# w_down by Strassen's seven products, and the sums of a second block moved from GpSimd to VectorE and ScalarE

## The chip, the cores and the metric

One Trainium2 chip, one of its cores. The metric is the device time of one execution in microseconds (us). Five engines work side by side, each through its own queue in order: TensorE (PE in the profile, its weight loads PEld), VectorE (DVE), ScalarE (ACT), GpSimd (POOL) and SyncE (SP), which issues the DMAs.

## The reference, cut to what matters

Two transformer blocks on 1024 tokens of width 1024, all in float32. The first block has two layers with windowed attention and an mLSTM and is not touched by the change. The second block mixes four branches, projects them, and ends in a feed-forward with squared ReLU:

```
y_a = diff_attention(q, k, v); y_b = conformer_conv(hb)
y_c = fourier_mix(hc);         y_d = spatial_gate(hd)
x   = x + concat(y_a, y_b, y_c, y_d) @ w_out
xn2 = rmsnorm(x, norm2_g)
x   = x + square(relu(xn2 @ w_up)) @ w_down     # 1024x1024 @ 1024x4096, then @ 4096x1024
out = rmsnorm(x, final_g)
```

## The kernel before, in words

Every float32 matrix product is made of three matmuls on split operands (`mm3`, lines 244 to 247): a value is cut into a high part, rounded by ScalarE to a reduced float32 type (line 250, or 266 for weights), and a low part, the difference, which VectorE subtracts (line 251, or 267). In `weights` the subtraction goes to GpSimd while `self.wpool` is set.

The second block's mixers are `block2`. `conformer_conv` (line 1505) is 60 VectorE multiply-adds over 1024 elements, fed in the background of the projections. `fourier_dft8` (1685, 1695) and `fourier_out` (1713) make the butterflies of the Fourier branch on GpSimd; the results are split for matmuls (251, into `xc`). `wpool` is set from the start of `block2`. `diff_attention` has 32 steps (4 heads by 8 query blocks): scores, a masked maximum on VectorE (1924), exp on ScalarE (1926), and in `diff_combine` the difference of two softmaxes: a scalar (1935) and then, in 16 of the 32 steps (`COMBINE`), a scaling (1937) and an add (1938) on GpSimd, in the others one VectorE instruction (1940). `stacks` (1798) makes 16 copies, half on ScalarE and half on GpSimd (`STACK`).

The feed-forward is `block3`. `up` multiplies by w_up with Strassen's seven products: tokens and hidden columns are cut in two, and the table `UP` lists for each product m which blocks of tokens and of weights are added or subtracted and to which of the four output blocks (token half, column half) the result goes with which sign. A product is 8 units (j) of 24 matmuls, 128x128 by 128x512. The sums of weights (2042) and of tokens (2026) are made on GpSimd, and the weights of the next unit are prepared while a unit is multiplied (`ahead`). Results gather in SBUF, the first by a ScalarE copy (2076), later ones by a VectorE add from PSUM (2079); a finished block goes through ReLU and square (2083, 2084) and to the DRAM tensor `hd` (2085).

`down` multiplies by w_down directly: two token halves (t), 16 pairs of 128 hidden columns (f), and for each pair 4 row tiles by 2 column halves by 2 by 3 = 48 matmuls of 128x512 into 8 PSUM banks. Per pair SP loads 512 KB of `hd` (2100) and twice 512 KB of w_down (2106); three operands of 128x1024 are split. Then the residual `x4` is loaded, PSUM is added (2139), and `rms_row` (470, 465, 1383) makes the output, which is stored (2141).

```
for t in range(2):
    ps = [self.pg.get() for _ in range(8)]
    for f in range(0, 32, 2):
        o = operands(t, f)
        ...
        for tt in range(4):
            for c in range(2):
                product(ps[2 * tt + c], o, tt, c)
```

The raw operands of `up` and `down` pass through `raw`, a ring of 6 buffers of 128x1024 (2 in `fa`, 4 in `t816a`), in order: a load into a buffer waits for the last reader of that buffer; `hd` has two buffers of its own in `down`. The split operands lie in 3 slots (`rwh`, `rwl`) and, for w_down, 4 pairs in `xa`.

What sets the order of the work: `block2`, `block3` and the projection before them stand in `tc.block(schedule_with_timeline_sim=True)`. A planner simulates the engines at build time and writes each engine's queue from the instructions that are ready; during execution every queue runs strictly in that order.

Of the kernel before, what the change touches and what calls it, by code (L numbers as in the profile page):

```python
# [73 lines left out]
STACK = "apap"  # L74
# [117 lines left out]
class Kernel:  # L192
# [1244 lines left out]
    def block2(self):  # L1437
# [9 lines left out]
        self.wpool = True  # L1447
# [24 lines left out]
        self.rate = 0  # L1472
        self.ph, self.pg, self.pt = self.banks(0), self.banks(1), self.banks(2, 3)
# [207 lines left out]
    def fourier_dft8(self, X):  # L1681
# [3 lines left out]
        TT = lambda o, a, b, op: nc.gpsimd.tensor_tensor(o, a, b, op=op)  # L1685
# [9 lines left out]
        TS = lambda o, a, x: nc.gpsimd.tensor_scalar(o, a, x, 0.0, op0=ALU.mult, op1=ADD)  # L1695
# [14 lines left out]
    def fourier_out(self, Sf, yT):  # L1710
        nc = self.nc
        ADD, SUB = ALU.add, ALU.subtract
        TT = lambda o, a, b, op: nc.gpsimd.tensor_tensor(o, a, b, op=op)
# [70 lines left out]
    def stacks(self, h, m, out):  # L1784
# [144 lines left out]
    def diff_combine(self, d):  # L1929
# [87 lines left out]
    def up_tokens(self, m):  # L2017
# [13 lines left out]
    def up_weights(self, m, j, raw):  # L2031
# [9 lines left out]
        if op:  # L2041
            self.nc.gpsimd.tensor_tensor(rs[0].ap, rs[0].ap, rs[1].ap, op=op)  # L2042
# [4 lines left out]
    def up(self, cur, raw, ahead):  # L2047
        nc, V = self.nc, self.nc.vector
        self.pg = self.banks(0, 1, 2, 3, 4, 5, 6, 7)
        cs = self.T(0, 512, 36, Slots)  # L2050
# [4 lines left out]
        acc = {}  # L2055
        units = [(m, j) for m in range(7) for j in range(8)]
        nxt = None
        for i, (m, j) in enumerate(units):
            if i + 1 < len(units):
                ahead.append(self.up_weights(*units[i + 1], raw))  # L2060
# [5 lines left out]
            w = ahead.pop(0)  # L2066
            for a in range(2):
# [4 lines left out]
                f = 2 * j + a  # L2072
                for c, sign in self.UP[m][4]:
                    if (c, f) not in acc:
                        acc[c, f] = [cs.get(), left[c]]
                        nc.scalar.activation(acc[c, f][0].ap, p.ap, AF.Copy, scale=float(sign))  # L2076
                    else:
                        o = acc[c, f][0].ap
                        V.tensor_tensor(o, o, p.ap, op=ALU.add if sign > 0 else ALU.subtract)  # L2079
                    acc[c, f][1] -= 1  # L2080
                    if not acc[c, f][1]:
                        o = acc.pop((c, f))[0]
                        nc.scalar.activation(o.ap, o.ap, AF.Relu)  # L2083
                        nc.scalar.activation(o.ap, o.ap, AF.Square)  # L2084
                        nc.sync.dma_start(self.hd[16 * c[1] + f, :, c[0] * 512:c[0] * 512 + 512], o.ap)
                        cs.free(o)
            self.done([w])

    def down(self, raw):

        nc, V, A = self.nc, self.nc.vector, self.A
        rw = Ring(self.xa, [4096 + 1024 * i for i in range(4)] + [1024 * i for i in range(4)], 1024)
        rres = self.T(0, 1024, 4)
        self.rny = self.F(1024, 1024, 2)
        fg = self.F(0, 1024, 1).get()
        nc.sync.dma_start(fg.ap, A["final_g_2"].unsqueeze(0).broadcast_to([128, 1024]))

        def operands(t, f):
            r = self.rraw.get([128, 2, 512])
            nc.sync.dma_start(r.ap, self.hd[f:f + 2, :, t * 512:t * 512 + 512].rearrange("f p t -> p f t"))  # L2100
            hid = self.rwh.get([128, 2, 512]), self.rwl.get([128, 2, 512])
            self.split(hid[0].ap, hid[1].ap, r.ap)
            ws = []
            for i in range(2):
                r = raw.get()
                nc.sync.dma_start(r.ap, A["w_down_2"][0][(f + i) * 128:(f + i) * 128 + 128])
                w = rw.get(), rw.get()
                self.split(w[0].ap, w[1].ap, r.ap)
                ws.append(w)
            return f, hid, ws  # L2110

        def product(p, o, tt, c):
            f, (hh, hl), ws = o
            ts, cols = slice(tt * 128, tt * 128 + 128), slice(c * 512, c * 512 + 512)
            for i, (wh, wl) in enumerate(ws):
                self.mm3(p.ap, hh[:, i, ts], hl[:, i, ts], wh[:, cols], wl[:, cols], f + i == 0, f + i == 31)

        for t in range(2):
            ps = [self.pg.get() for _ in range(8)]
            last = []  # L2120
            for f in range(0, 32, 2):
                o = operands(t, f)
                if f >= 28 and t == 1:
                    last.append(o)
                    continue
                for tt in range(4):
                    for c in range(2):
                        product(ps[2 * tt + c], o, tt, c)
                self.done([o[1]])
            for tt in range(4):  # L2130
                rows = slice(t * 512 + tt * 128, t * 512 + tt * 128 + 128)
                x = rres.get()
                nc.sync.dma_start(x.ap, self.x4[rows])
# [60 lines left out]
```

## Time and profile before

| what | value |
|---|---|
| median of 3 runs | 2839.69 us (2837.2 to 2842.19) |
| the profiled execution | 2835.86 us; span of its profile 2834.1 us |
| PE busy | 2666.5 us, 94% |
| DVE, ACT, POOL busy | 1723.9, 1410.3, 725.0 us |
| DMA | 307.99 MB, mean 109 GB/s |

How to read the rows: in rows of windows a stretch is followed by its length, then busy us and (instructions) of PE, PEld, DVE, ACT and POOL, the granted TensorE clock (1.00 is the upper of its two levels, 2.4 GHz; 0.5 would be the lower, 1.2 GHz; a value between is a mix over the stretch), the DMA engines' busy share and GB/s. Matmuls are pipelined, so the time of one in a full stream is the stretch divided by their number, not the duration shown for one.

### The profile page before, as it was taken

How to read it: one execution, taken by the hardware profiler on the slowest of the kernel's cores; microseconds unless marked ns; L12 is line 12 of the kernel's file. 1: busy time of each engine (PE TensorE's matmuls, PEld its weight loads, DVE VectorE, ACT ScalarE, POOL GpSimd, SP SyncE). 2: the span in 40 equal slices, each digit the busy share in tenths (PEclk: the TensorE clock that was granted, in tenths of full speed). 3: DMA queues.
4: the chain of work that ended last, by engine and by line, in shares of the span. 5: the costliest groups of instructions: out<-in, count | busy, mean ns of one | idle time of the engine just before them, and what ended most of it. 6: DMA issues, size and time to landing. Idle time of an engine off the chain costs nothing. (4 is left out here: it accounts for less than half of the span.)

```text
span 2834.1 us, 44013 instructions
## 1 busy us (share of the span) xinstructions
PE 2666.5 (94%) x16414; PEld 2312.6 (82%) x16414; DVE 1723.9 (61%) x3530; ACT 1410.3 (50%) x3039; POOL 725.0 (26%) x810
## 2 busy tenths in 40 slices
PE   7999989999999999999998887898899999999998
PEld 3888878898889787888988877688798887888887
DVE  4788755646756788666455469788824475633433
ACT  4666545546525666556463252476705626632332
POOL 0122203414200122123131149265501544200000
PEclk9999999999999999999999988999999999999999
DMA  7101021112554101112215440423235666854542
GB/s 246 29 15 56 26 56 46 51 50 77 166 181 146 49 23 50 32 51 67 61 58 158 132 148 23 128 96 101 84 98 169 209 201 217 295 174 138 208 142 89
DMA packets 285859, 307.99 MB, mean 109 GB/s; under 512 B 17904, under 2 KB 242508, under 8 KB 285388
## 3 DMA queue, kind: packets, MB, share of 16 engines
q1 hardware_dynamic: 285644, 305.17, 34.1%
q8 instruction: 129, 2.11, 0.3%
q14 instruction: 86, 0.70, 0.1%
HBM read 249.70 MB, written 55.42 MB: 108 GB/s over the span
## 5 line engine op out<-in xcount | busy, mean ns | idle before, releaser
L245 PE MATMUL psum<-xa 128*128 128x512 f32 (+2 forms) x2200 | 779.8, 356 | 13.4 <-ACT xa L250 6.7
L246 PE MATMUL psum<-xa 128*128 128x512 f32 (+2 forms) x2200 | 775.4, 353 | 4.3 <-POOL xa L267 3.0
L247 PE MATMUL psum<-xa 128*128 128x512 f32 (+2 forms) x2200 | 773.4, 352 | 5.4 <-DVE xa L251 4.6
L245 PEld LDWEIGHTS psum<-xa 128*128 128x128 f32 x2200 | 421.6, 192 | 68.6 <-ACT xa L250 7.7
L247 PEld LDWEIGHTS psum<-xa 128*128 128x128 f32 x2200 | 421.3, 191 | 58.8 <-DVE xa L251 6.6
L246 PEld LDWEIGHTS psum<-xa 128*128 128x128 f32 x2200 | 421.9, 192 | 56.5 <-POOL xa L267 3.2
L465 POOL TENSOR_TENSOR rsb<-rsa,half 128x1 f32<-128x1 f32 (+1 forms) x129 | 90.0, 698 | 780.8 <-DVE rsa L463 723.5
L245 PE MATMUL psum<-xa,xg 128*128 128x256 f32 (+1 forms) x864 | 248.8, 288 | 1.7 <-DVE fa L1523 1.1
L247 PE MATMUL psum<-xa,xg 128*128 128x256 f32 (+1 forms) x864 | 245.7, 284 | 0.0
L246 PE MATMUL psum<-xa,xg 128*128 128x256 f32 (+1 forms) x864 | 245.7, 284 | 0.0
L251 DVE TENSOR_TENSOR xa<-fa,xa 128x1024 fp32r<-128x1024 f32 (+2 forms) x121 | 139.2, 1162 | 165.3 <-ACT xa L250 165.1
L806 POOL TENSOR_SCALAR fa<-fa,esk 128x640 f32<-128x640 f32 (+2 forms) x144 | 112.2, 792 | 450.9 <-DVE esk L804 361.2
L251 DVE TENSOR_TENSOR xa<-t816a,xa 128x1024 fp32r<-128x1024 f32 x84 | 115.1, 1372 | 175.5 <-ACT xa L250 171.9
L266 ACT ACTIVATE xa<-fa 128x1024 fp32r<-128x1024 f32 (+1 forms) x104 | 109.9, 1059 | 189.2 <-PE psum L247 109.9
L250 ACT ACTIVATE xa<-fa 128x1024 fp32r<-128x1024 f32 (+2 forms) x121 | 112.4, 942 | 171.5 <-PE psum L247 63.7
L267 DVE TENSOR_TENSOR xa<-fa,xa 128x1024 fp32r<-128x1024 f32 (+1 forms) x84 | 103.2, 1230 | 125.3 <-ACT xa L266 120.9
L250 ACT ACTIVATE xa<-t816a 128x1024 fp32r<-128x1024 f32 x84 | 88.3, 1054 | 167.4 <-PE psum L247 108.2
L245 PEld LDWEIGHTS psum<-xa,xg 128*128 128x128 f32 x864 | 163.9, 190 | 3.0 <-DVE fa L1523 1.5
L246 PEld LDWEIGHTS psum<-xa,xg 128*128 128x128 f32 x864 | 163.6, 189 | 0.7 <-issue 0.7
L247 PEld LDWEIGHTS psum<-xa,xg 128*128 128x128 f32 x864 | 163.5, 189 | 0.4 <-issue 0.3
L245 PE MATMUL psum<-xg,xa 128*128 128x512 f32 x376 | 154.1, 411 | 1.3 <-ACT xa L266 0.5
L247 PE MATMUL psum<-xg,xa 128*128 128x512 f32 x376 | 152.0, 405 | 2.7 <-POOL xa L267 2.7
(498 smaller groups left out, 6023.9 us busy)
## 6 DMA issues: line engine op xcount, KB each, us to landing
fa<-in_w_in_dram SPq DMA_DIRECT2D x64, 512.0 KB
t816a<-in_w_up_dram SPq DMA_DIRECT2D x64, 512.0 KB
fa<-in_w_ada_dram SPq DMA_DIRECT2D x48, 512.0 KB
t816a<-in_w_down_dram SPq DMA_DIRECT2D x44, 512.0 KB
fa<-in_w_up_dram SPq DMA_DIRECT2D x32, 512.0 KB
hd<-t816a SPq DMA_DIRECT2D x64, 256.0 KB
fa<-hd SPq DMA_DIRECT2D x32, 512.0 KB
fa<-in_w_out_dram SPq DMA_DIRECT2D x24, 512.0 KB
```

The costliest lines, as they stand in the source:

```text
L245: mm(out, lh, rh, start=start, stop=False)
L246: mm(out, lh, rl, start=False, stop=False)
L247: mm(out, ll, rh, start=False, stop=stop)
L250: self.nc.scalar.activation(hi, src, AF.Copy)
L251: self.nc.vector.tensor_tensor(lo, src, hi.bitcast(F32), op=ALU.subtract)
L266: self.nc.scalar.activation(h.ap, r.ap, AF.Copy)
L267: (self.nc.gpsimd if self.wpool else self.nc.vector).tensor_tensor(l.ap, r.ap, h.ap.bitcast(F32), op=ALU.subtract)
L465: self.nc.gpsimd.tensor_tensor(r, e, self.half.broadcast_to([128, m]), op=ALU.pow)
L806: nc.gpsimd.tensor_scalar(P[j][:, :nk], P[j][:, :nk], e[:, j:j + 1], 0.0, op0=ALU.mult, op1=ALU.add)
```

## The change

Five things. (1) `down` uses the seven products of the table `DOWN` (token halves and hidden halves; hidden halves and output-column halves): 7 products of 8 units of 24 matmuls into 4 banks each. A unit has one hidden factor and one weight factor of 128x1024, each possibly a sum of two blocks made on VectorE; two units are prepared ahead. (2) The hidden blocks of the second token half stay in SBUF (`self.H`); only the first half goes to `hd`. (3) The residual is loaded whole into `x`, and every product's result is added to the one or two places that its table row names. (4) In `up` the sums of weights and tokens move from GpSimd to VectorE, and the weights are prepared two units ahead instead of one; the accumulators are pairs of 512 columns. (5) In the second block the Fourier sums go to VectorE and its scalings to ScalarE, the low parts of weights before the attention to VectorE, half of the stack copies to ScalarE, the softmax scaling of 16 steps to ScalarE, and a VectorE instruction with two tensor inputs (1935) becomes one with one.

```diff
-STACK = "apap"
@@ block2
-        self.wpool = True
         next(zin[0])
...
         self.rate = 0
+        self.wpool = True
         self.ph, self.pg, self.pt = self.banks(0), self.banks(1), self.banks(2, 3)
@@ fourier_dft8 and fourier_out
-        TT = lambda o, a, b, op: nc.gpsimd.tensor_tensor(o, a, b, op=op)
+        TT = lambda o, a, b, op: nc.vector.tensor_tensor(o, a, b, op=op)
-        TS = lambda o, a, x: nc.gpsimd.tensor_scalar(o, a, x, 0.0, op0=ALU.mult, op1=ADD)
+        TS = lambda o, a, x: nc.scalar.activation(o, a, AF.Copy, scale=x)
@@ stacks
-            if STACK[h] == "a":
-                nc.scalar.activation(s[:96], f[:96], AF.Copy)
-            else:
-                nc.gpsimd.tensor_scalar(s[:96], f[:96], 1.0, 0.0, op0=ALU.mult, op1=ALU.add)
+            nc.scalar.activation(s[:96], f[:96], AF.Copy)
@@ diff_combine
-        V.scalar_tensor_tensor(r[:, 1:2], sm[:, 0:1], r[:, 1:2], self.nlam, op0=ALU.mult, op1=ALU.mult)
+        V.tensor_scalar(r[:, 1:2], r[:, 1:2], sm[:, 0:1], self.nlam, op0=ALU.mult, op1=ALU.mult)
-            nc.gpsimd.tensor_scalar(P[1].ap, P[1].ap, r[:, 1:2], 0.0, op0=ALU.mult, op1=ALU.add)
+            nc.scalar.activation(P[1].ap, P[1].ap, AF.Copy, scale=r[:, 1:2])
@@ up_tokens and up_weights
-                self.nc.gpsimd.tensor_tensor(r.ap, *src, op=op)
+                self.nc.vector.tensor_tensor(r.ap, *src, op=op)
-            self.nc.gpsimd.tensor_tensor(rs[0].ap, rs[0].ap, rs[1].ap, op=op)
+            self.nc.vector.tensor_tensor(rs[0].ap, rs[0].ap, rs[1].ap, op=op)
@@ up
+        ahead.append(self.up_weights(*units[1], raw))
-            if i + 1 < len(units):
-                ahead.append(self.up_weights(*units[i + 1], raw))
+            if i + 2 < len(units):
+                ahead.append(self.up_weights(*units[i + 2], raw))
...
+                    if c[0]:
+                        self.H[c, j] = o
+                    else:
+                        f = 16 * c[1] + 2 * j
+                        nc.sync.dma_start(self.hd[f:f + 2].rearrange("f p t -> p f t"), o.ap)
+                        self.cs.free(o)
+    DOWN = [
+        ([(0, 0), (0, 1)], ALU.add, [(1, 1)], None, [((0, 0), -1), ((0, 1), 1)]),
+        ([(0, 0)], None, [(0, 1), (1, 1)], ALU.subtract, [((0, 1), 1), ((1, 1), 1)]),
+        ([(0, 0), (1, 1)], ALU.add, [(0, 0), (1, 1)], ALU.add, [((0, 0), 1), ((1, 1), 1)]),
+        ([(0, 1), (1, 1)], ALU.subtract, [(1, 0), (1, 1)], ALU.add, [((0, 0), 1)]),
+        ([(1, 1)], None, [(1, 0), (0, 0)], ALU.subtract, [((0, 0), 1), ((1, 0), 1)]),
+        ([(1, 0), (1, 1)], ALU.add, [(0, 0)], None, [((1, 0), 1), ((1, 1), -1)]),
+        ([(1, 0), (0, 0)], ALU.subtract, [(0, 0), (0, 1)], ALU.add, [((1, 1), 1)]),
+    ]
@@ down
+        def factor(rs, op, h, l):
+            if op:
+                r = rs[0][0] if rs[0][1] else rs[1][0] if rs[1][1] else raw.get([128, 2, 512])
+                V.tensor_tensor(r.ap, rs[0][0].ap, rs[1][0].ap, op=op)
+            else:
+                r = rs[0][0]
+            self.split(h.ap, l.ap, r.ap)
...
+            for i in range(2):
+                self.mm3(p.ap, hh[:, i, ts], hl[:, i, ts], wh[:, i], wl[:, i], j + i == 0, j == 7 and i == 1)
+        units = [(m, j) for m in range(7) for j in range(8)]
+        ahead = [operands(*u) for u in units[:2]]
...
+                for (t, n), sign in self.DOWN[m][4]:
+                    y = x[4 * t + tt][:, n * 512:n * 512 + 512]
+                    V.tensor_tensor(y, y, ps[tt].ap, op=ALU.add if sign > 0 else ALU.subtract)
+                if m in (4, 6):
+                    t = 4 * (m == 6) + tt
+                    self.rms_row(x[t].ap, fg.ap)
+                    nc.sync.dma_start(A["out"][t * 128:t * 128 + 128], x[t].ap)
```

`operands(m, j)` loads each hidden block with t = 0 from `hd` and each weight block (256 rows by 512 columns) into a buffer of `raw`, 512 KB a load, and calls `factor` for the hidden and the weight side. A hidden block with t = 1 comes from `self.H` without a load.

## Rows read from the trace of the kernel before

**Rows 1.** The page, part 1: busy time, share of the span, instructions.
```profile
PE 2666.5 (94%) x16414; PEld 2312.6 (82%) x16414; DVE 1723.9 (61%) x3530; ACT 1410.3 (50%) x3039; POOL 725.0 (26%) x810
```
**Rows 2.** Windows: start of block 2, attention, up, down, and one full stretch of down.
```profile
1680.00:1800.00 120.00, 100.94 (x532) 87.02 (x530) 114.80 (x84) 34.76 (x80) 83.41 (x47) 0.91 0.15 46
...
1720.00:1840.00 120.00, 92.87 (x461) 77.73 (x460) 104.80 (x103) 40.44 (x83) 70.77 (x47) 0.87 0.27 84
1860.00:2060.00 200.00, 178.96 (x1336) 163.24 (x1335) 161.36 (x314) 138.22 (x256) 114.00 (x79) 0.97 0.29 88
2160.00:2480.00 320.00, 313.33 (x1362) 257.32 (x1362) 182.68 (x198) 175.63 (x264) 125.72 (x50) 0.98 0.69 224
2480.00:2826.00 346.00, 346.00 (x1528) 286.42 (x1526) 127.52 (x122) 101.76 (x110) 3.86 (x7) 1.00 0.44 150
...
2500.00:2600.00 100.00, 100.00 (x443) 82.84 (x442) 34.71 (x30) 30.84 (x31) 0.00 (x0) 1.00 0.44 148
```
**Rows 3.** Groups by line, VectorE, from 2480 us on (count, busy, mean ns).
```profile
L251 DVE TENSOR_TENSOR xa<-fa,xa 128x1024 fp32r<-128x1024 f32 x50 | 60.3, 1222 | 111.4 <-ACT xa L250 111.4
...
L2139 DVE TENSOR_TENSOR t816a<-t816a,psum 128x512 f32<-128x512 f32 x16 | 10.7, 685 | 9.2 <-PE psum L247 9.2
L1383 DVE SCALAR_TENSOR_TENSOR t816a<-t816a,rsb,fa 128x1024 f32<-128x1024 f32 x8 | 10.2, 1280 | 1.5 <-POOL rsb L465 1.5
```
**Rows 4.** The same stretch, ScalarE: the high parts.
```profile
L250 ACT ACTIVATE xa<-fa 128x1024 fp32r<-128x1024 f32 x50 | 51.6, 1050 | 121.3 <-PE psum L247 63.4 <-DMA fa<-hd 51.0 <-DMA fa<-in_w_down_dram 6.9
```
**Rows 5.** Timeline, VectorE: subtractions that follow one another (start, us).
```profile
2503.92 1.22 DVE L251 TENSOR_TENSOR xa<-fa,xa 128x1024 fp32r<-128x1024 f32 x1
2505.06 1.22 DVE L251 TENSOR_TENSOR xa<-t816a,xa 128x1024 fp32r<-128x1024 f32 x1
```
**Rows 6.** DMA issues of down by tile: hidden and weight loads.
```profile
L2100 SPq DMA_DIRECT2D fa<-hd x32: 359/377/447, 2456.7 to 2785.5; - x32
...
L2106 SPq DMA_DIRECT2D t816a<-in_w_down_dram x44: 327/328/423, 2445.0 to 2775.8; - x44
L2106 SPq DMA_DIRECT2D fa<-in_w_down_dram x20: 328/328/425, 2479.6 to 2774.6; - x20
```
**Rows 7.** Windows: the stretch with the longest stall in up, and up's last loads.
```profile
2260.00:2280.00 20.00, 17.39 (x70) 13.89 (x69) 16.09 (x19) 5.59 (x6) 11.01 (x5) 0.91 0.53 170
...
2460.00:2470.00 10.00, 10.00 (x46) 8.29 (x45) 5.32 (x8) 6.87 (x11) 0.00 (x0) 1.00 0.95 348
```
**Rows 8.** Timeline in up: two loads issued by SP, and GpSimd's sum of them.
```profile
2321.80 0.92 SPq L2038 DMA_DIRECT2D t816a<-in_w_up_dram  x2
...
2327.28 2.38 POOL L2042 TENSOR_TENSOR t816a<-t816a 128x1024 f32<-128x1024 f32 x1 [5.51 <-DMA t816a<-in_w_up_dram]
```
**Rows 9.** Groups by line, GpSimd, from 1500 us on: most sums of w_up.
```profile
L2042 POOL TENSOR_TENSOR t816a<-t816a 128x1024 f32<-128x1024 f32 x26 | 63.8, 2456 | 105.0 <-DMA t816a<-in_w_up_dram 73.1 <-DVE xa L251 17.1 <-issue 8.2
```
**Rows 10.** Timeline at 1775 us: VectorE and GpSimd side by side.
```profile
1775.73 2.57 DVE L251 TENSOR_TENSOR xc<-fa,xc 128x256 fp32r<-128x256 f32 x1
...
1775.49 2.53 POOL L267 TENSOR_TENSOR xa<-fa,xa 128x1024 fp32r<-128x1024 f32 x1
```
**Rows 11.** Groups by line and shape, VectorE, 1540 to 2110 us.
```profile
L1505 DVE SCALAR_TENSOR_TENSOR t604a<-t604a,cols 128x1024 f32<-128x1024 f32 x60 | 105.8, 1765 | 2.5 <-ACT t604a L1502 1.3
...
L1935 DVE SCALAR_TENSOR_TENSOR drs<-dsm,drs,nlam 128x1 f32<-128x1 f32 x32 | 12.6, 393 | 0.6
L251 DVE TENSOR_TENSOR xc<-t604a,xc 128x256 fp32r<-128x256 f32 x17 | 11.8, 709 | 0.0
...
L251 DVE TENSOR_TENSOR xc<-fa,xc 128x256 fp32r<-128x256 f32 x7 | 7.2, 1031 | 0.0
...
L251 DVE TENSOR_TENSOR xc<-psum,xc 128x256 fp32r<-128x256 f32 x2 | 0.7, 414 | 0.0
```
**Rows 12.** Timeline, VectorE: four multiply-adds of line 1505 with GpSimd idle.
```profile
1792.52 5.25 DVE L1505 SCALAR_TENSOR_TENSOR t604a<-t604a,cols 128x1024 f32<-128x1024 f32 x4
```
**Rows 13.** Who PE waited for, 1660 to 1860 us: the longest.
```profile
PE psum L246 <- DVE xc L251: 11.5, 6, 8.1
```

More of the change, by code (lines that the diff above doesn't have):

```diff
@@ L2049, in up @@
         self.pg = self.banks(0, 1, 2, 3, 4, 5, 6, 7)
[L2050 removed]
+        self.cs = self.T(0, 1024, 18, Slots)
         left = {}
@@ L2066, in up @@
             w = ahead.pop(0)
+            outs = [(c, sign, (c, j) not in acc) for c, sign in self.UP[m][4]]
+            for c, _, first in outs:
+                if first:
+                    acc[c, j] = [self.cs.get([128, 2, 512]), left[c]]
             for a in range(2):
@@ L2071, in up @@
                     self.mm3(p.ap, w[0][:, k, c], w[1][:, k, c], h[:, k], l[:, k], k == 0, k == 3)
[L2072 to L2076, printed above, removed]
+                for c, sign, first in outs:
+                    o = acc[c, j][0][:, a]
+                    if first:
+                        nc.scalar.activation(o, p.ap, AF.Copy, scale=float(sign))
@@ L2112, in product @@
[L2112 to L2119, printed above, removed]
-            last = []
[L2121 to L2124, printed above, removed]
+        rx = self.F(0, 1024, 8)
@@ new lines, in down @@
+        x = [rx.get() for t in range(8)]
+        for t in range(8):
+            nc.sync.dma_start(x[t].ap, self.x4[t * 128:t * 128 + 128])
+        fg = self.F(8192, 1024, 1).get()
+        nc.sync.dma_start(fg.ap, A["final_g_2"].unsqueeze(0).broadcast_to([128, 1024]))
+        self.rny = Ring(self.ta, [s[1] for s in self.cs.free_[:2]], 1024)
+        def factor(rs, op, h, l):
[5 more added lines that the diff above has]
+            self.split(h.ap, l.ap, r.ap)
@@ new lines, in operands @@
+        def operands(m, j):
+            ab, aop, bb, bop, _ = self.DOWN[m]
+            rs = []
+            for t, c in ab:
+                if t:
+                    rs.append((self.H[(t, c), j], False))
+                else:
+                    r = raw.get([128, 2, 512])
+                    f = 16 * c + 2 * j
+                    nc.sync.dma_start(r.ap, self.hd[f:f + 2].rearrange("f p t -> p f t"))
+                    rs.append((r, True))
+            hid = self.rwh.get([128, 2, 512]), self.rwl.get([128, 2, 512])
+            factor(rs, aop, *hid)
+            rs = []
+            for c, n in bb:
+                r = raw.get([128, 2, 512])
+                f = (16 * c + 2 * j) * 128
+                nc.sync.dma_start(
+                    r.ap, A["w_down_2"][0][f:f + 256, n * 512:n * 512 + 512].rearrange("(f p) c -> p f c", p=128))
+                rs.append((r, True))
+            w = rw.get([128, 2, 512]), rw.get([128, 2, 512])
+            factor(rs, bop, *w)
+            return hid, w
@@ new lines, in product @@
+        def product(p, o, j, tt):
+            (hh, hl), (wh, wl) = o
+            ts = slice(tt * 128, tt * 128 + 128)
+            for i in range(2):
+                self.mm3(p.ap, hh[:, i, ts], hl[:, i, ts], wh[:, i], wl[:, i], j + i == 0, j == 7 and i == 1)
+        units = [(m, j) for m in range(7) for j in range(8)]
+        ahead = [operands(*u) for u in units[:2]]
+        todo = units[2:]
+        for m in range(7):
+            ps = [self.pg.get() for _ in range(4)]
+            last = []
+            for j in range(8):
+                if todo and not last:
+                    ahead.append(operands(*todo.pop(0)))
+                o = ahead.pop(0)
+                if m == 6 and j >= 6:
+                    last.append((j, o))
@@ L2125, in down @@
                     continue
                 for tt in range(4):
-                    for c in range(2):
-                        product(ps[2 * tt + c], o, tt, c)
-                self.done([o[1]])
+                    product(ps[tt], o, j, tt)
+                self.done([o[0]])
             for tt in range(4):
-                rows = slice(t * 512 + tt * 128, t * 512 + tt * 128 + 128)
-                x = rres.get()
-                nc.sync.dma_start(x.ap, self.x4[rows])
-                for c in range(2):
-                    p = ps[2 * tt + c]
-                    for o in last:
-                        product(p, o, tt, c)
-                    cols = slice(c * 512, c * 512 + 512)
-                    V.tensor_tensor(x[:, cols], x[:, cols], p.ap, op=ALU.add)
@@ L2140, in down @@
-                self.rms_row(x.ap, fg.ap)
-                nc.sync.dma_start(A["out"][rows], x.ap)
-            self.done([o[1] for o in last])
+                for j, o in last:
+                    product(ps[tt], o, j, tt)
+                for (t, n), sign in self.DOWN[m][4]:
[5 more added lines that the diff above has]
+                    nc.sync.dma_start(A["out"][t * 128:t * 128 + 128], x[t].ap)
@@ L2144, in run @@
+        self.done([o[0] for _, o in last])
     def run(self):
```

34 lines of the change are left out of this document (9 added, 25 removed).

## Prediction

> **What bounds the kernel now.** I read the page's busy times first, then windows by stage, then groups and timelines of the stages that the change touches. TensorE is busy 94% of the span, VectorE 61% [rows 1]: PE is the bound on average, and what is left is found by stage [rows 2]. In down PE is never idle: 346 us of 346, clock 1.00, a full stretch holding 443 matmuls per 100 us, so 0.2257 us each. Its 2 x 16 x 48 = 1536 matmuls make 346.7 us, and VectorE is 37% busy beside them. In up PE is idle 6.7 of 320 us and loses 0.02 of the clock, 6.4 us: 13.1 us together, with DMA at 69%. At the start of block 2 VectorE is the full engine: busy 114.8 of 120 us from 1680 us on, with GpSimd at 83.4; from 1720 us on PE idles 27.1 of 120 us and the clock stands at 0.87, 15.6 us more. The attention has PE at 179, VectorE at 161 and ScalarE at 138 of 200 us.
>
> **The change part by part.**
>
> *Down, matmuls.* 7 products x 8 units x 24 = 1344 of the same shape, 192 fewer. 192 x 0.2257 = **-43.3 us**, if PE stays full.
>
> *Down, what has to hide beside them.* A unit lasts 24 x 0.2257 = 5.42 us.
> VectorE: before, a 48-matmul pair cost three subtractions. Now each unit has two, and sums: one in m = 0, 1, 4, 5, two in m = 2, 3, 6. A subtraction of 1024 takes 1.22 us, and a sum has the same shape, so the same; 48 adds from PSUM at 0.685 and 8 output rows at 1.28 come on top [rows 3]. The high parts, 1.05 us on ScalarE [rows 4], are no load: 2.1 us a unit. Subtractions that follow one another start 1.14 us apart, the 1.22 overlapping [rows 5]. So all down: (112 + 80) x 1.14 + 48 x 0.685 + 8 x 1.28 = 262 us of 303. The heaviest, m = 2 (32 instructions and 8 adds): 36.5 + 5.5 = 42.0 of 43.4 us. It fits with little to spare.
>
> Here a rule of the Trainium skill speaks against the change: "VectorE: DVE Perf Modes", section "The DRAIN you can't avoid", says that an instruction starts only when the pipe of the one before is empty. By it m = 2 would be 32 x 1.22 + 5.5 = 44.5 us, above its 43.4, and m = 2 and 3 would cost some 2 us together. The timeline shows starts 1.14 us apart, so I keep that.
>
> DMA: loads of 512 KB. 3 per unit in m = 0, 1, 2, 3, 6, 2 in m = 4, 1 in m = 5: 18 x 8 = 144 against 32 + 64 = 96 before [rows 6]. Three in 5.42 us are 290 GB/s; up reached 348 GB/s at 0.95 share for 10 us [rows 7], so they fit at some 80% share. SP's issues (0.33 to 0.38 us, 144 of them) are 52 us of 303.
>
> The ring of raw buffers is tighter. Six buffers at three a unit: each must come round every 2 units, 10.84 us; before, w_down had six at two per 10.84 us. From issue to use of a pair took 5.5 us [rows 8]. Then 1.14 (sum) + 1.05 + 1.22 + 0.4 (issue): 9.3 us, 1.5 to spare. In these rows two loads were together, here three. Lower bound 0, since split operands are prepared two units ahead. Upper bound: three more VectorE instructions queued ahead of the release, 12.7 us a turn, 6.37 a unit: 0.95 x 40 units = 38 us. A third price: if VectorE's queue put each subtraction straight behind its own sum, it would stand idle for ScalarE's 1.05 us, and a two-sum unit would take 6.66 instead of 5.42 us: 24 x 1.24 = 30 us. I take **+8 us**: nearest to the row of 9.3, with something for bursts at m = 2 and 3.
>
> *Handover from up to down.* The first units' loads wait for raw buffers that up's last weights leave; two units of lookahead stand against 5.5 us of landing. Bounds 0 and 5.5, **+2 us**. The eight loads of x wait on SP for the last reader of the token buffer, with w_up's loads queued behind; that reader is some ten units before the end, and the planner knows it: in the 2. At the end the chain after the last matmul (add, square, power, scale, store) stays: 0.
>
> *Up.* 40 + 10 sums leave GpSimd (2.46 us each [rows 9]) for VectorE at 1.22: 61 us on 183 busy of 320, so 76%, not the bound. Loads get one more unit of time, the sum shortens by 1.2 us, stores to hd halve. Bounds: all 13.1 us back, or one more stall like the worst (2.6 us idle and 0.09 x 20 = 1.8 us of clock, 4.4 us [rows 7]). **-5 us**.
>
> *Start of block 2.* While GpSimd works, VectorE's own instructions with two SBUF inputs stretch: a 256-column subtraction that ends with GpSimd's instruction took 2.57 us [rows 10], from PSUM it takes 0.41; the 60 multiply-adds took 1.765 each [rows 11] against 5.25/4 = 1.31 with GpSimd idle [rows 12]. So what leaves VectorE is 60 x 0.45 = 27 us and 17 x 0.30 + 7 x 0.62 = 9 us of Fourier splits, 36 us; what comes is Fourier's 4 x 1.22 + 8 x 0.68 + 20 x 0.41 = 18.5 us and some 7 low parts of weights at 1.22, 8.5 us: 27 us (the scalings, 8 of 256 columns, go to ScalarE, 29% busy). Net 9 us less on the engine that is full. Bounds: +27, if nothing of the stretching goes, since VectorE is full; -43, if PE's idle time and clock loss go wholly. PE's longest wait there is for the Fourier splits, up to 8.1 us at once [rows 13], which stand behind GpSimd's chain and the multiply-adds. **-10 us**, VectorE's net.
>
> *Attention.* ScalarE gets 16 scalings and 8 copies at 1.05: 25 us on 138 of 200 (over all of the attention, some 220 us). They queue behind exps, and the add on GpSimd waits for the scaling; two steps of lag hide that. VectorE loses at most the 12.6 us that line 1935 takes now [rows 11], and the stretching by GpSimd's 16 scalings and 8 copies. Bounds: +25, all of ScalarE's on the path; -27, PE's 21 us idle and 6 us of clock back. Gain and loss lie on engines of like load: **0**.
>
> *Sum.* -43.3 + 8 + 2 - 5 - 10 = -48.3 us on the profiled execution's 2835.86 (span 2834.1 and 1.8 around it): 2787.6. The median stands 3.8 us above that execution, so **2791.4 us**.
>
> **The rivals.**
> A, *the raw ring starves PE* (slower). Place: m = 0 to 3 and 6; it decides from a turn of 10.84 us. For: three loads a unit at 80% of the DMA, six buffers. Against: 9.3 us from rows, and up's ring lost only 13 us. Price: a turn of 13.4 us makes each of 40 units 1.3 us late, 52 us, and in up's worst stretch each idle us took 0.7 us of clock with it [rows 7]: 36 more. 2791.4 - 8 + 88 = 2871. The turn at which the whole change gives nothing: the 56 us of gain over 40 x 1.7 is 0.83 us a unit, 12.5 us.
> B, *VectorE paces the two-sum units*, subtraction straight behind its sum: 30 us for 8, 2813. For: 42.0 of 43.4 us. Against: in up other instructions fill such gaps.
> C, *the lock goes and takes the stalls with it*: GpSimd's instructions keep VectorE out, so Fourier's chain and the multiply-adds hold PE, and with them gone block 2's 43 us and up's 13 come back: 2791.4 - 33 - 8 = 2750, and 8 less if down is full too, 2742. The Trainium skill, "SBUF — State Buffer", section "SBUF: two separate sides", calls it an exclusive lock held for a whole instruction; the timeline agrees (2.57 beside 2.53 us), and by that rule alone C would be the forecast. Against: VectorE stays nearly full with the work that comes.
> D, *block 2 does not do what is meant*: the planner lays the sums ahead of what PE waits for; VectorE's 27 us come and no relief: 2791.4 + 10 + 27 = 2828.
>
> **How the numbers follow.** Forecast (2765 to 2812) 0.60, A 0.08, B 0.12, C 0.12, D 0.08. The range 2758 to 2826 holds the forecast, B, half of D and a part of C (a relief that comes only in part); it leaves out A, the rest of C and of D, some 0.2. A measurement can tell about 0.2%, 5.7 us, from no change. Slower: A beyond 2845 and a little of D with stalls in down, 0.08. Same: the rest of D and the small A, 0.05. Faster 0.87.
>
> **What would show it.** Right: some 443 matmuls per 100 us through down, lasting 303 to 315 us; VectorE near 87% there and DMA at 75 to 85%; multiply-adds of line 1505 near 1.31 us; fewer waits of PE for the Fourier splits. Wrong: PE waiting for splits in every unit of m = 2, 3 or 6 with SP waiting for VectorE's release (A), VectorE idle for ScalarE between sum and subtraction (B), a start of block 2 longer than before with PE waiting for VectorE (D). If VectorE's sums take 2.4 us, as on GpSimd, the forecast falls.

## The result and the profile after

The changed kernel takes **2797.23 us** (median of 4 runs, 2795.17 to 2800.55) against 2839.73 for the kernel before beside it (4 runs): ratio 0.9852, 95% interval 0.9834 to 0.9869. Predicted: 2791.4, range 2758 to 2826. The profiled execution took 2799.03 us, span 2797.3.

The page, part 1, of the kernel after, beside [rows 1]:
```profile
PE 2630.7 (94%) x16222; PEld 2277.3 (81%) x16222; DVE 1865.4 (67%) x3750; ACT 1449.1 (52%) x3023; POOL 481.5 (17%) x686
```
192 matmuls are gone, GpSimd is busy 244 us less, VectorE 141 us more. The rest does not show in shares of the span, so the span is cut where the stages begin (their first instructions in the two traces; for the scores, the first masked maximum; for down, the matmul behind up's 1344; "down" ends with its last matmul):

| from, to | before | after | difference | predicted |
|---|---|---|---|---|
| start to the Fourier branch's input copy (the same code but for three low parts of weights) | 1676.1 | 1672.8 | -3.3 | |
| to the first scores | 147.5 | 118.1 | -29.4 | -10 |
| to the first add behind w_out | 243.4 | 255.7 | +12.3 | 0 |
| to up's first matmul | 89.8 | 89.9 | +0.2 | 0 |
| up | 321.1 | 319.4 | -1.7 | -5 |
| down | 348.3 | 333.4 | -14.9 | -33.3 |
| tail | 7.9 | 7.9 | 0 | 0 |

The same windows as [rows 2], with up and down cut at their new bounds:
```profile
1680.00:1800.00 120.00, 111.78 (x605) 94.91 (x603) 112.49 (x131) 46.77 (x102) 4.74 (x2) 0.96 0.31 95
...
2140.00:2456.00 316.00, 308.98 (x1351) 252.91 (x1350) 214.17 (x244) 163.18 (x195) 0.54 (x1) 0.99 0.65 209
2456.00:2789.00 333.00, 314.98 (x1345) 254.93 (x1343) 256.76 (x252) 126.84 (x129) 7.83 (x7) 0.98 0.67 222
2700.00:2740.00 40.00, 40.00 (x178) 33.15 (x177) 32.17 (x35) 17.35 (x21) 6.71 (x4) 1.00 0.60 201
```
Down was full before; now TensorE idles 18.0 of its 333 us, and its clock is 0.98. A full stretch (the last row) still takes 0.225 us a matmul, and a product without a stall 43.5 us, so 7 x 43.5 = 304.5 us would do. The 28.9 above it are idle time and, in the stretches behind it, the lower clock. They are not spread evenly: the seven products lasted 50.5, 49.1, 50.7, 48.6, 44.0, 43.5 and 47.0 us.

What is late is read from who waited for whom, down only (total us, times, longest). TensorE:
```profile
PE psum L246 <- DVE xa L250: 17.2, 12, 3.6
```
VectorE:
```profile
DVE t816a L2119 <- DMA t816a<-hd: 30.8, 20, 5.7
DVE t816a L2119 <- DMA t816a<-in_w_down_dram: 21.3, 10, 5.4
DVE fa L2119 <- DMA fa<-in_w_down_dram: 15.1, 9, 4.6
...
DVE xa L250 <- ACT xa L249: 3.1, 3, 1.5
```
TensorE waits for low parts (line 250) that VectorE subtracts, and VectorE stands 67.2 us in front of sums (line 2119) whose blocks have not landed. Its timeline at the first seam between products (start, us, and in brackets the idle time before) shows what such a wait does, and a second suspect beside it:
```profile
2504.97 1.23 DVE L2119 TENSOR_TENSOR fa<-fa 128x1024 f32<-128x1024 f32 x1 [4.60 <-DMA fa<-in_w_down_dram]
...
2508.78 1.22 DVE L250 TENSOR_TENSOR xa<-fa,xa 128x1024 fp32r<-128x1024 f32 x1
2509.91 1.22 DVE L250 TENSOR_TENSOR xa<-t816a,xa 128x1024 fp32r<-128x1024 f32 x1
...
2516.77 3.67 DVE L2176 TENSOR_TENSOR fa<-fa,psum 128x512 f32<-128x512 f32 x6
2520.36 1.22 DVE L250 TENSOR_TENSOR xa<-t816a,xa 128x1024 fp32r<-128x1024 f32 x1
2521.50 1.22 DVE L250 TENSOR_TENSOR xa<-fa,xa 128x1024 fp32r<-128x1024 f32 x1
2522.63 1.22 DVE L2119 TENSOR_TENSOR t816a<-t816a 128x1024 f32<-128x1024 f32 x1
```
The wait of 4.60 us holds every subtraction queued behind it. The six PSUM additions in one go stand right ahead of the subtraction for which TensorE waited 3.06 us:
```profile
2521.63 0.50 PE L246 MATMUL psum<-xa 128*128 128x512 f32 x1 [3.06 <-DVE xa L250]
```
So two theories were tried: **L**, loads come late to sums that stand early in VectorE's queue; **P**, the bursts of additions use up the lead.

### The profile page after: what moved, and what is told of

The parts are those of the page before. It is cut to its first block, busy times and chain, and to the rows that moved or that the text cites. A ratio compares the mean times of both kernels' runs of the same rounds, so it can differ in the third digit from the quotient of the medians.

```text
span 2797.3 us, 43718 instructions
## 1 busy us (share of the span) xinstructions
PE 2630.7 (94%) x16222; PEld 2277.3 (81%) x16222; DVE 1865.4 (67%) x3750; ACT 1449.1 (52%) x3023; POOL 481.5 (17%) x686
## 5 line engine op out<-in xcount | busy, mean ns | idle before, releaser
L246 PE MATMUL psum<-xa 128*128 128x512 f32 (+2 forms) x2136 | 751.4, 352 | 25.5 <-DVE xa L250 24.5
L244 PE MATMUL psum<-xa 128*128 128x512 f32 (+2 forms) x2136 | 757.5, 356 | 13.1 <-ACT xa L249 5.0
L245 PE MATMUL psum<-xa 128*128 128x512 f32 (+2 forms) x2136 | 751.2, 352 | 0.9 <-DVE xa L266 0.8
L246 PEld LDWEIGHTS psum<-xa 128*128 128x128 f32 x2136 | 408.8, 191 | 84.5 <-DVE xa L250 34.5
L244 PEld LDWEIGHTS psum<-xa 128*128 128x128 f32 x2136 | 409.9, 192 | 66.9 <-ACT xa L249 6.4
L245 PEld LDWEIGHTS psum<-xa 128*128 128x128 f32 x2136 | 409.1, 192 | 50.5 <-DVE xa L266 1.6
L249 ACT ACTIVATE xa<-t816a 128x1024 fp32r<-128x1024 f32 x125 | 131.0, 1056 | 206.6 <-DVE t816a L2119 110.9
L266 DVE TENSOR_TENSOR xa<-fa,xa 128x1024 fp32r<-128x1024 f32 (+1 forms) x94 | 115.3, 1229 | 133.6 <-ACT xa L265 123.1
L250 DVE TENSOR_TENSOR xa<-t816a,xa 128x1024 fp32r<-128x1024 f32 x125 | 151.3, 1219 | 21.2 <-ACT xa L249 13.1
L244 PE MATMUL psum<-xg,xa 128*128 128x512 f32 x376 | 153.2, 408 | 3.9 <-DVE fa L1764 2.8
L246 PE MATMUL psum<-xg,xa 128*128 128x512 f32 x376 | 151.7, 404 | 1.0 <-POOL xa L266 1.0
L245 PE MATMUL psum<-xg,xa 128*128 128x512 f32 x376 | 152.1, 404 | 0.2 <-DVE xg L250 0.2
L1008 DVE SCALAR_TENSOR_TENSOR fa<-fa,vec 128x640 f32<-128x640 f32 (+2 forms) x128 | 110.5, 869 | 51.7 <-ACT fa L1006 50.5
```

The costliest lines, as they stand in the source:

```text
L244: mm(out, lh, rh, start=start, stop=False)
L245: mm(out, lh, rl, start=False, stop=False)
L246: mm(out, ll, rh, start=False, stop=stop)
L249: self.nc.scalar.activation(hi, src, AF.Copy)
L250: self.nc.vector.tensor_tensor(lo, src, hi.bitcast(F32), op=ALU.subtract)
L266: (self.nc.gpsimd if self.wpool else self.nc.vector).tensor_tensor(l.ap, r.ap, h.ap.bitcast(F32), op=ALU.subtract)
```

## The experiments

Three sets of four, each beside the kernel before on its chip (2844.07, 2842.73 and 2841.19 us, 7 runs each). Ratios are to that kernel; the changed kernel's is 0.9852. Stage lengths are read from each trace as above.

**Down alone.** Parts (4) and (5) of the change undone (of (4), the accumulators stay in pairs).
```diff
+        self.wpool = True
         next(zin[0])
-        TT = lambda o, a, b, op: nc.vector.tensor_tensor(o, a, b, op=op)
+        TT = lambda o, a, b, op: nc.gpsimd.tensor_tensor(o, a, b, op=op)
...
-            self.nc.vector.tensor_tensor(rs[0].ap, rs[0].ap, rs[1].ap, op=op)
+            self.nc.gpsimd.tensor_tensor(rs[0].ap, rs[0].ap, rs[1].ap, op=op)
```


> The new down alone; block 2 and up's GpSimd sums and lookahead of one as before. By the stages of the two traces (block 2 and all ahead of up 20 us shorter, up 2, down 15) down is worth 15 us: 2825 us (2819 to 2831), with down lasting some 333 us. Rival, that the parts don't add since the planner lays the whole block anew: anything that is not 2825, and if the 20 us ahead of up are chance and not block 2's edits, about 2805.

Measured 2825.08 us, ratio 0.9941 (0.9918 to 0.9964). The total is the one expected, but not by the stages expected: down lasts 327.0 us and not some 333, and the part up to the Fourier branch's input copy, 1682.6 us, is 6.5 longer than in the kernel before. Down's own instructions are those of the changed kernel, so down alone differs by 6 us between planned kernels, and smaller differences between such kernels say nothing below.

**Block 2 alone.** Part (5) put into the kernel before (the first half of the diff above, the other way round, with the stacks, the scaling and line 1931).

> Block 2's edits alone; up and down as before. Theory (GpSimd's instructions kept VectorE out, and with them gone PE no longer waits for the Fourier splits): 2820 us (2814 to 2826), attention starting some 30 us earlier and lasting some 10 us longer. Rival (VectorE's net of 9 us is all there is to gain, as the prediction took): 2830. Rival (chance of the planner's layout): 2836 to 2844.

Measured 2820.78 us, ratio 0.9921 (0.9906 to 0.9936). -19 and -23 us make the whole change's -42, with next to nothing left for part (4), which is in neither run: in the total the parts add up (by stages down gives 21 us alone and 15 in the whole change), so each can be studied by itself.

**Additions written later.** A product's PSUM additions are written behind the next product's first four units.
```diff
                 self.done([o[0]])
+                if late:
+                    late.pop(0)()
...
+                if m < 6:
+                    late.append(lambda tt=tt, f=finish: f(tt))
+                else:
+                    finish(tt)
```


> The changed kernel, but each product's adds from PSUM are issued one row tile at a time after the next product's first four units, not all together at its end. Theory P (the adds at a product's end, six of them 3.7 us in one go, stand ahead of the subtraction that PE waits for): the stalls of 3.1, 3.6 and 3.1 us after m = 0, 1, 2 go, with the clock lost behind them: 12 to 17 us faster than the changed kernel, 2780 to 2785. Theory R (raw buffers turn over too slowly, VectorE waits for loads and has no lead when the adds come): 0 to 4 us, 2793 to 2797.

Measured 2804.07 us, ratio 0.9855 (0.9834 to 0.9875). It tells nothing of P: the planner put the six additions back together (VectorE's timeline of this kernel):
```profile
2519.85 3.67 DVE L2177 TENSOR_TENSOR fa<-fa,psum 128x512 f32<-128x512 f32 x6
```

**Eight raw buffers.** Two more in down, from the ring of split weights (3 pairs for 4).
```diff
-        rw = Ring(self.xa, [4096 + 1024 * i for i in range(4)] + [1024 * i for i in range(4)], 1024)
+        rw = Ring(self.xa, [4096 + 1024 * i for i in range(4)] + [0, 1024], 1024)
...
+        raw.slots, raw.i = raw.slots[k:] + raw.slots[:k] + [[None, s[1], self.ta] for s in self.cs.free_[:2]], 0
```


> The changed kernel with eight raw buffers in down instead of six (two come from the accumulators that are free by then; split weights have 3 pairs instead of 4). Theory R: VectorE's 67 us of waiting for loads shrink by more than half, PE's stalls in m = 0, 1, 2 mostly go: 12 to 22 us faster than the changed kernel, 2775 to 2785. Theory P: VectorE's waits shrink, but the bursts of adds stall PE as before after m = 0, 1, 2: 4 to 9 us faster, the stalls of m = 0 alone, 2788 to 2793. Theory V (VectorE is simply full): no change.

Measured 2808.68 us, ratio 0.9875 (0.9854 to 0.9897), down 335.5 us; up, planned in the same block, lasts 327.3 us, 7.9 more than in the changed kernel. Two more buffers gain nothing in this order, at the price of a pair of split weights: VectorE still waits some 70 us in front of sums, as in the changed kernel (the two largest of its waits in this kernel's down):
```profile
DVE t816a L2121 <- DMA t816a<-in_w_down_dram: 31.3, 17, 4.7
DVE fa L2121 <- DMA fa<-in_w_down_dram: 12.9, 6, 4.3
```

**One load for each side.** Where a sum has two blocks from DRAM, this kernel leaves the second out and adds the first to itself.
```diff
-                if t:
+                if any(o for _, o in rs) and not t:
+                    rs.append(rs[0])
+                elif t:
                     rs.append((self.H[(t, c), j], False))
...
             for c, n in bb:
+                if rs:
+                    rs.append(rs[0])
+                    continue
```


> The changed kernel with one load for each side of a unit of down: where a sum had two blocks from DRAM, the first is summed with itself (so the second blocks of the sums are left out of the product). VectorE, ScalarE and TensorE do the same work, and SP issues 32 + 80 minus the 8 x 9 or so second loads. Changed kernel beside it: about 2797 to 2802 us, down 333 us long against 305 of matmuls. Theory L (VectorE stands in its queue in front of sums whose loads have 4.5 to 5.5 us from issue to landing and are issued only when a split has released the raw buffer): down loses 12 to 18 us, 2782 to 2788, and VectorE's waits on transfers in down (67 us now) fall below 25. Theory P (six PSUM additions of 680 ns in one go eat the lead at the end of products 0 to 2, whatever the loads do): the three TensorE waits of 3.1 to 3.6 us stay, time within 4 us of the changed kernel.

Measured 2784.71 us, ratio 0.9796 (0.9778 to 0.9814); down 311.1 us, products of 43.5 to 46.6. VectorE's waits for transfers:
```profile
DVE t816a L2119 <- DMA t816a<-hd: 12.9, 9, 3.6
DVE t816a L2119 <- DMA t816a<-in_w_down_dram: 10.0, 9, 3.4
...
DVE fa L2119 <- DMA fa<-in_w_down_dram: 7.1, 7, 2.2
DVE fa L2119 <- DMA fa<-hd: 5.0, 3, 2.6
```
35.0 us, not the 25 expected, but 22 of the 28.9 us in down are gone with VectorE's work unchanged. L stands. (Fewer loads also turn the ring less often, so this run alone doesn't part L from rival A; the runs in written order below do, with six buffers and all the loads.)

**Additions of four products off VectorE.** They become copies on ScalarE; this kernel leaves out what the rows held before.
```diff
-                    V.tensor_tensor(y, y, ps[tt].ap, op=ALU.add if sign > 0 else ALU.subtract)
+                    if m < 4:
+                        nc.scalar.activation(y, ps[tt].ap, AF.Copy)
+                    else:
+                        V.tensor_tensor(y, y, ps[tt].ap, op=ALU.add if sign > 0 else ALU.subtract)
```


> The changed kernel with the 28 PSUM additions of down's products 0 to 3 made copies on ScalarE into the same rows (so the earlier content of the rows and the sum over those products are left out): 28 x 0.68 = 19 us leave VectorE, and PSUM is released by ScalarE, which is busy 127 of 333 us there. Loads, sums and splits stay. Theory P: the TensorE waits of 3.1 to 3.6 us behind the ends of products 0, 1 and 2 go, and the low clock behind them: down 10 to 16 us shorter, 2784 to 2790. Theory L: VectorE waits for transfers instead of adding, the waits stay or move, time within 4 us of the changed kernel (2797 to 2802).

Measured 2811.45 us, ratio 0.9893 (0.9878 to 0.9907): slower, which neither theory expected. In its trace 8.8 of the 11.9 us come ahead of the Fourier branch's input copy and 3.9 in up; down is 336.1 us, no shorter than in the changed kernel where P expected 10 to 16 us less. What VectorE no longer adds it waits (same view):
```profile
DVE t816a L2119 <- DMA t816a<-hd: 38.5, 23, 4.7
DVE t816a L2119 <- DMA t816a<-in_w_down_dram: 25.4, 15, 4.2
DVE fa L2119 <- DMA fa<-in_w_down_dram: 21.7, 11, 4.5
```
85.6 us, 18.4 more than in the changed kernel. VectorE was not short of time in down; P falls as the main cause.

**Down in its own order.** Down's loop in a block of its own, without the planner's simulated timeline, the additions written later as above.
```diff
         todo = units[2:]
+        yield
+        late = []
         for m in range(7):
...
-            self.block3()
+            d = self.block3()
+            next(d)
+        with self.tc.block():
+            next(d, None)
...
```


> The same work as the changed kernel; down's loop over products stands in a block of its own whose instructions are issued in the order in which they are written, and the PSUM additions of a product are written behind the next product's first four units, one or two a unit (VectorE's queue then holds sum, subtraction, subtraction, one or two additions, and so on, where the planner put six additions in one go). Costs 1 to 3 us at the seam of the blocks. Theory P: products 1 to 3 lose their starting waits, down 8 to 14 us shorter, 2786 to 2793. Theory L: VectorE still meets each sum's loads late; within 4 us of the changed kernel.

Measured 2787.98 us, ratio 0.9803 (0.9787 to 0.982); down 315.3 us with all the loads, products of 43.5, 43.5, 45.6, 48.4, 47.0, 43.5 and 43.7. VectorE's queue now holds sums, subtractions and pairs of additions by turns, and its waits for transfers in down are 34.9 us. A part of its timeline, and the window of down:
```profile
2551.42 1.22 DVE L2118 TENSOR_TENSOR t816a<-t816a 128x1024 f32<-128x1024 f32 x1
2552.56 1.22 DVE L250 TENSOR_TENSOR xa<-t816a,xa 128x1024 fp32r<-128x1024 f32 x1
2553.69 1.27 DVE L2177 TENSOR_TENSOR fa<-fa,psum 128x512 f32<-128x512 f32 x2
...
2462.00:2777.00 315.00, 307.38 (x1343) 250.99 (x1341) 255.16 (x249) 123.91 (x127) 5.88 (x7) 1.00 0.72 239
```
By what was written down beforehand this result spoke for P (8 to 14 us), and against L (no gain); the next run parts the two. The tail behind the last matmul is 9.7 us in this and the other kernels in written order, 1.9 longer.

**The same, additions not moved.** As the kernel above without the hunk that moves them.

> Control of the kernel with down in a block of its own: the same block, but the PSUM additions of a product written where the changed kernel has them, behind its last matmuls, so that they may stand in one go. What it shares with that kernel: sums, subtractions and loads follow the written order of units and not the planner's. If the place of the sums is what gained the 18 us of down (333 to 315), this one has them too: down 313 to 320 us, 2786 to 2793. If the spread of the additions is what gained, its products 1 to 3 show the TensorE waits of some 3 us again: down 325 to 333 us, 2796 to 2804.

Measured 2789.86 us, ratio 0.9815 (0.98 to 0.983); down 314.6 us, though eight additions stand in one go (VectorE), and TensorE waits behind them:
```profile
2555.45 4.86 DVE L2176 TENSOR_TENSOR fa<-fa,psum 128x512 f32<-128x512 f32 x8
...
2566.05 0.50 PE L245 MATMUL psum<-xa 128*128 128x512 f32 x1 [1.81 <-DVE xa L250]
...
2614.51 0.79 PE L245 MATMUL psum<-xa 128*128 128x512 f32 x1 [1.82 <-DVE xa L250]
```
Behind the bursts that end products 1 and 2 TensorE waits 1.81 and 1.82 us, and the next products last 47.9 and 48.4 us; spread, the additions make products 2 to 4 as much longer (above). So 18 of the 28.9 us are the order of the queues, and spreading the bursts gains nothing. (Against the 327.0 us of the kernel with down alone it is 12.)

**Loads a unit ahead, eight buffers.** Down in its own order, additions later, and two more raw buffers as above; besides:
```diff
+            ra, rs = got.pop(0)
+            if more:
+                got.append(loads(*more.pop(0)))
             hid = self.rwh.get([128, 2, 512]), self.rwl.get([128, 2, 512])
```


> As the kernel with down in its written order and the additions spread, and besides 8 raw buffers in place of 6 (two more, taken from the ring of split weights, which gets 3 pairs for 4) and the loads of a unit written one unit ahead of its sums, so that SP issues them some 5 us earlier. Theory L: loads are there when VectorE comes to the sum; VectorE's waits on transfers below 20 us, products of 43.5 to 45 us, down 310 to 318 us, 2780 to 2787. Theory P alone: same time as the kernel with the written order and 6 buffers, within 3 us. If the ring of 3 pairs of split weights binds (VectorE's splits wait for TensorE to release one), slower than that kernel by 3 to 8 us.

Measured 2788.15 us, ratio 0.9812 (0.9791 to 0.9832). Down is 311.6 us, in the range expected by L, but VectorE's waits for transfers are 34.6 us and not below 20, and the total is that of six buffers: up, still planned, lasts 328.6 us against 320.6, spread over its products, as in the planned kernel with eight buffers.

**Attention's edits undone.** In the changed kernel, `STACK`, the scaling and line 1931 as before.
```diff
-            nc.scalar.activation(P[1].ap, P[1].ap, AF.Copy, scale=r[:, 1:2])
+            nc.gpsimd.tensor_scalar(P[1].ap, P[1].ap, r[:, 1:2], 0.0, op0=ALU.mult, op1=ALU.add)
```


> The changed kernel with attention's two edits undone: the second stack of every pair of heads and the scaling of the second exponential by lambda are GpSimd's again; the Fourier part's mixing stays on VectorE and ScalarE. Attention (first to last maximum of scores) took 229.7 us in the changed kernel and 221.6 before, with ScalarE busy 175.6 and 155.2 us of it. Theory S (ScalarE's 20 us more stand on attention's path): attention 4 to 9 us shorter than in the changed kernel, 2790 to 2796. Theory N (attention is longer because the Fourier part's own work now falls into it, its start being 33 us earlier): no gain, 2797 to 2803. GpSimd's lock back (VectorE's instructions in attention longer): slower by 3 to 10 us.

Measured 2803.66 us, ratio 0.9863 (0.9848 to 0.9877): no gain. From the first scores to the first add behind w_out it takes 257.3 us (255.7 in the changed kernel). The windows of this stretch in the kernel before, the changed one and this one:
```profile
1824.00:2067.00 243.00, 220.03 (x1567) 198.03 (x1567) 190.20 (x373) 161.88 (x293) 128.25 (x91) 0.96 0.29 92
...
1791.00:2047.00 256.00, 228.81 (x1571) 204.79 (x1572) 195.54 (x386) 184.43 (x318) 101.39 (x67) 0.94 0.28 88
...
1796.00:2054.00 258.00, 234.65 (x1571) 211.04 (x1572) 208.72 (x387) 161.84 (x294) 129.17 (x91) 0.90 0.28 87
```
TensorE's idle time does go back (23.4 us; 27.2 in the changed kernel, 23.0 before), but the clock falls to 0.90 and VectorE is busy 13 us more. So giving ScalarE's work back doesn't shorten the stretch; whether that work alone lengthened it is not shown, since GpSimd's instructions came back with it.

**Up and down in their own order.** The block's seam put ahead of `up`, additions later, six buffers.
```diff
         self.rtmp = raw
+        yield
         self.up(first, raw, ahead)
         self.down(raw)
```


> The changed kernel with up and down both in a block of their own in written order, 6 raw buffers, additions of down behind the next product's first units. Up has 319.6 us for 1344 matmuls of 0.2267 us (304.7), of which some 9 us are TensorE's waits for splits (lowest stretch 146 matmuls in 40 us). If the planner's order is what costs up too: up 308 to 314 us and down 313 to 317, 2778 to 2784. If up's waits come from elsewhere (the PSUM additions of up wait for TensorE in VectorE's queue, in front of the next unit's sums): up 320 to 335 us, 2788 to 2803.

Measured **2773.05 us**, ratio 0.9764 (0.9737 to 0.9791). Windows of up and of down in this kernel:
```profile
2150.00:2452.00 302.00, 302.00 (x1334) 250.07 (x1333) 218.99 (x249) 167.04 (x197) 0.00 (x0) 1.00 0.71 227
2453.00:2763.00 310.00, 306.32 (x1344) 251.44 (x1342) 251.78 (x246) 119.49 (x123) 5.86 (x6) 1.00 0.71 232
```
Up is full, at a clock of 1.00, 305.3 us for its 1344 matmuls: the planner's order had cost it nearly all that it lost. The two stages are 37 us shorter than in the changed kernel, more than was expected, the span 25: up's first matmul comes 10.8 us later in this trace, 6.7 of it already at the Fourier branch's input copy, where the code is the same, and 4.8 between the first add behind w_out and the seam; the tail is 1.9 longer. So some 7 of the 37 us are paid for at the two ends of the new block.

**The same, loads a unit ahead, eight buffers in down.**

> The kernel with up and down in their written order, and in down 8 raw buffers, 3 pairs of split weights and the loads written a unit ahead of the sums (which alone had down 311.6 against 315.3 us, but started it some 4 us later at the seam between the blocks). With the seam ahead of up those 4 us should not appear: 2 to 5 us less than the kernel with 6 buffers and both in written order. If the later start came from the loads themselves (eight raw buffers taken from up's last units), the two are equal within 2 us.

Measured 2774.34 us, ratio 0.9758 (0.9736 to 0.978): equal to the kernel with six buffers. In its trace up lasts 305.4 us, so eight buffers lengthen it only where it is planned, and the gain in down is there, 307.2 against 310.3 us, with products of 43.5 to 44.8:
```profile
2448.00:2755.00 307.00, 305.06 (x1343) 251.50 (x1342) 248.25 (x244) 120.68 (x124) 5.13 (x7) 1.00 0.70 229
```
Three us of 2774 are too few for these runs to tell apart. Both kernels beat the changed one; their intervals lie clear of its.

## Why the prediction was right, and where it was not

The time fell into the range, 5.8 us above the forecast, with two terms off: up and down together 21.7 us worse than predicted, block 2 7.1 us better, and 3.3 us came ahead of nearly everything changed. That makes 11.5 us between the two profiled executions. In the medians 5.6 of them don't show: the first execution stood 3.8 us below its median, which the forecast added, and the second stands 1.8 above its own. That the forecast is off by only 5.8 us is partly luck: half of what up and down missed was made up for by errors the other way. By the signs that the prediction named, down was not as foreseen: 333.4 us and not 303 to 315, VectorE 77% busy and not 87, DMA 67% and not 75 to 85.

*Down's matmuls*, -43.3: right. A product without a stall lasts 43.5 us, as 192 x 0.2257 = 43.3 said.

*Down's stalls and the handover*, +8 and +2: mis-sized, 28.4 us where 10 were taken, and for a wrong reason. The step that failed was the ring, "9.3 us, 1.5 to spare", as the thing that could be late. Eight buffers in a planned order gained nothing (335.5 us); the same six buffers in the written order took 315.3. The 1.5 to spare were not there either: the 5.5 us in that sum are one row, while the sum at 2504.97 above waited for this load of SP, 6.8 us old by then:
```profile
2498.13 0.37 SPq L2142 DMA_DIRECT2D fa<-in_w_down_dram  x1
```
For the loads that an engine waited for in the changed kernel's down, issue to landing was 3.6 to 7.3 us; with 7.3 the turn is 11.1 us, above its 10.84. The row that would have told is [rows 8], with [rows 9]: GpSimd stood 5.5 us in front of one sum, and 73 us in all, for w_up's loads. I used the 5.5 us as a time to land and did not ask what stands behind the waiting sum. On GpSimd nothing of haste did; on VectorE the subtractions do. What VectorE waited for in up, in the kernel before:
```profile
DVE xa L251 <- ACT xa L250: 122.9, 46, 8.1
DVE t816a L2079 <- PE psum L247: 11.9, 11, 2.0
```
And in the kernel after:
```profile
DVE t816a L2038 <- DMA t816a<-in_w_up_dram: 51.1, 19, 4.9
DVE xa L250 <- ACT xa L249: 22.4, 14, 4.5
DVE fa L2038 <- DMA fa<-in_w_up_dram: 18.1, 10, 4.6
```
With the sums, their waits for loads moved to VectorE, in up and in down. *Up* therefore gave 1.7 us where I took 5; in the written order it gives 15.8 (321.1 to 305.3), of which 4.8 are lost again at the seam ahead of it. My bound of 13.1 from [rows 2] was a little short, since that window leaves out up's first 3 us.

That a wait for a load goes over to the subtractions behind it is read from the timelines; that the order of the queues is what lets it reach TensorE is shown: the planner's order, with the same work, buffers and loads, costs 18 to 23 us in down (12 to 17 against the shortest planned down, 327.0) and 14 in up. Which instructions stand wrong in it was not tried one by one. Why the planner sets the sums so early (it may count on loads that land sooner) is not shown.

*VectorE's work*: 262 us predicted for down, 256.8 measured. The sums took 1.22 us, as the subtractions. The prediction set the rule of the Trainium skill ("VectorE: DVE Perf Modes", "The DRAIN you can't avoid") against the trace, as an instruction that starts only when the pipe of the one before is empty; the same section goes on that a next instruction that is not held starts earlier. The trace shows the second: 2521.50, 2522.63 in the timeline above are 1.13 us apart at 1.22 each. Product 2 ran in 43.5 us in the kernel with both stages in written order.

*Rival A* (the ring starves TensorE) had the symptom, SP waiting for VectorE's subtractions to release buffers (149 us in down). Eight buffers didn't help, though with a pair of split weights less; what decides is that SP waits as long (154 us) in the kernel with down in written order, where down takes 315.3 us with the same six buffers. *Rival B* (VectorE idle for ScalarE) fell: those waits are 3.1 us in the changed kernel's down and 16.3 us in the faster one with the written order.

*Start of block 2*, -10: mis-sized, -29.4 us. VectorE's groups of the changed kernel, beside [rows 11], and the longest of TensorE's waits from 1660 to 1860 us, beside [rows 13]:
```profile
L1504 DVE SCALAR_TENSOR_TENSOR t604a<-t604a,cols 128x1024 f32<-128x1024 f32 x60 | 80.6, 1351 | 0.8
...
L1931 DVE TENSOR_SCALAR drs<-drs,dsm,nlam 128x1 f32<-128x1 f32 x32 | 8.6, 269 | 0.4
L250 DVE TENSOR_TENSOR xc<-t604a,xc 128x256 fp32r<-128x256 f32 x17 | 6.8, 416 | 2.7 <-ACT xc L249 2.7
...
PE psum L1916 <- DVE dnm L1920: 4.3, 6, 2.0
```
The relief of VectorE came as counted (1351 against the 1310 ns expected, 416 against 709). I took VectorE's net of 9 us for the stage's gain; but VectorE is as busy as before (112.5 of 120 us), while TensorE now works 111.8 instead of 100.9 us, and the longest wait of [rows 13], for the Fourier splits, is gone. Whether that is because they no longer stand behind GpSimd's chain or because VectorE's instructions are shorter was not tried apart. *Rival C* was nearer for this stretch: 29.4 of its 43 us. Its rule (the Trainium skill, "SBUF — State Buffer", "SBUF: two separate sides") agrees with these durations; the total that it gave, 2742 to 2750, did not come, since up and down got waits of another kind. *Rival D* fell with the run of block 2 alone.

*Attention*, 0: wrong by 12.3 us, within its bounds. In the windows above TensorE is busy 228.8 instead of 220.0 us for the same matmuls (1571 and 1567), at a clock of 0.94 instead of 0.96, and idle 27.2 instead of 23.0. So two thirds are longer matmuls, of which the clock explains some 5 us (0.02 of 256); why it is lower, and how much is ScalarE's, is open.

## What to carry to other kernels

An instruction moved to another engine takes its waits with it: before moving a sum, look at what it waits for where it stands (here 5.5 us for loads on an engine with nothing urgent behind it), and at what will stand behind it in the new queue. When an engine is three quarters busy and yet late, ask for its order before its load: the same work in written order gave back 37 us of up and down (25 of the whole), where two more buffers or 19 us less work gave nothing. A gain that is worked out as the net of a full engine's work can be too small: count what the engine that sets the end waits for.

## What was not expected of the hardware

PSUM additions of 128x512 in one go take 3.67 us for six and 4.86 for eight, 0.6 us each, where a single one shows 0.68. The Fourier branch's input copy, with all but the same instructions ahead of it, started at 1672.8 to 1682.6 us in the traces of the changed kernel and its variants, so a stage is compared by its length, not by where it ends.
